# The store of the transposed input moved behind the first index-head rotation, and more urgent PSUM copies of the decays' sums

## The chip, the cores and the metric

The kernel runs on one core of one Trainium2 chip. TensorE (PE) multiplies matrices, VectorE (DVE), ScalarE (ACT) and GpSimd (POOL) work on elements, SyncE (SP) issues almost all DMA transfers. Each engine takes its instructions in one fixed order and waits by semaphores for the others. The time is that of one execution on the device, in microseconds.

## The reference

One layer of a hybrid streaming encoder for two groups of streams that share the weights: a prompt of 512 new frames and a sample group of 64 frames whose first 512 positions lie in a cache. The width is 1024.

```python
mod = (jax.nn.silu(c) @ w_ada + b_ada)[:, None, :]
sh1, sc1, gt1, sh2, sc2, gt2 = jnp.split(mod, 6, axis=-1)
h = rms_normalize(x) * g_norm_mix * (1.0 + sc1) + sh1
q, k, v, qi, ki, wi, z, xbc, dt, gate_logits = jnp.split(h @ w_in, offs, axis=-1)
q = rope(rms_normalize(q.reshape(b, t, N_HEADS, HEAD_DIM)) * g_q, pos)
k = rope(rms_normalize(k.reshape(b, t, N_KV_HEADS, HEAD_DIM)) * g_k, pos)
qi = rope(qi.reshape(b, t, IDX_HEADS, IDX_DIM), pos)
ki = rope(ki[:, :, None, :], pos)[:, :, 0, :]
...
score = jnp.einsum('th,ths->ts', ww.astype(jnp.float32), jax.nn.relu(logits))
score = jnp.where(kpos[None, :] < limit[:, None], score, -jnp.inf)
_, idx = lax.top_k(score, topk)
...
dtp = jax.nn.softplus((dt + dt_bias).astype(jnp.float32))
acs = jnp.cumsum(dtc * a.reshape(g, r), axis=2)
w_state = jnp.exp(acs[:, :, -1:] - acs) * dtc
...
mixed = (g_attn * (o_attn @ w_branch_attn) + g_ssm * (y @ w_branch_ssm)) @ w_out
x = x + gt1 * mixed
```

Eight index heads score all keys, each query keeps its best 128 (prompt) or 144 (sample), attention runs over these, a state-space scan (SSD) runs on another slice of the projection, and both branches are merged, projected and added to x. A SwiGLU block follows. The residual x is needed again near the end; the decays' sums (acs) are needed by the scan.

## The kernel before

The kernel is written as a plain program (`build`), in which every operation is recorded by a planner, `Plan`. Nothing is issued while the program is recorded. `order` then lists the operations: it keeps for each engine a heap of those whose inputs are ready, takes the one of highest urgency, and books a modelled duration (`cost`). The urgency is the place in the program minus an offset, which `with R.prio(n)` sets: `R.prio(4000)` makes an operation as urgent as one that stands 4000 operations earlier, `R.prio(-1500)` less urgent. `with R.after(ops)` adds dependencies for the planner only. `emit` issues everything in the resulting order, so each engine's queue, SyncE's too, is that order. All instructions therefore have one line, L533, in the profile, and are told apart by their tiles. Because one choice shifts all later ones, a small edit changes the order of many operations.

Memory is given out by pools. A pool opens and closes by events that stand in program order: "close" takes effect in the plan once all operations of the pool have been listed, and a later "open" waits behind it. Operations of a pool that isn't open are held. Memory of a closed pool goes to the next pool on its side; an operation on the new tile waits on the chip for the last users of the old one.

The stages around the change, in the order of the program (lines of the kernel before):

- Start (692 to 893). x is loaded (`xt`), normalized and transposed; the modulation's first 2048 columns are computed by `ada_pair`; `h_tile` makes the projection's input in two parts, high (`hTh`) and low (`hTl`), because each product is made of three fast ones. At urgency -1500, lines 870 to 883 transpose the raw x by TensorE into PSUM (`pxt`), copy it to five tiles `xs` in pool `xsp`, and store them to `x_d`, a scratch array in HBM, from which the residual is read near 924 us. These are six stores: four of 512 KB (rows of 512 bytes) and two of 128 KB (rows of 128 bytes).
- `R.close(sp, xsp)` at line 951, then pools "attn" and "index" open. Their first operations load the rope table `cs2`, the gains `gqk`, and for the index keys the cached part: `kd` (named `kisd`), inside `key_stack`. `key_stack` copies the rotated new keys beside the cached ones, transposes them (PSUM tag `px`), and splits them into high and low parts (`kis`, on ScalarE and VectorE).
- Index heads (1072 to 1078). For each half, `tm` projects four heads into `tok`, `rope` rotates them (two products on VectorE into `tmpb`, one on GpSimd, one addition on VectorE, whose operation is kept as `ropes[0]` or `ropes[1]`), and `q_stack` transposes and splits them into `qis`.
- Decays (1081 to 1129). Softplus on VectorE (tiles `e1`, `e2`, `e3`, shown as `e`), then sums by matmuls with a triangular matrix (`pacs` in a `px` bank) and with ones (`ptot` in a `py` bank). `nacs` is the negated first, `edec` the exponential of the second, `wst` their sum. The same sums transposed (`pacsT`) go to `acsT` and to HBM.
- Index scores and top-k (1132 to 1171). Per block of 128 queries: two matmuls per head into a `py` bank, ScalarE's relu into `lg`, VectorE's weighted sum into `score`, then 16 or 18 passes of the eight largest (`m`, by MAX8) and their removal (MATCH_REPLACE8), then a mask.
- Modulation, `ada_columns(4, adx)` (1174 to 1177, held back to `ropes[0]`): four loads `adr` from `w_ada`, 16 accumulations on VectorE (`aacc`), and a few matmuls. Pool "adax" lies on the right side of the memory.
- Keys `kx` and values `vx`: projection, and for the keys `rope` with a normalization (a sum of squares on VectorE into `rr`, a power on GpSimd, a product). Then the queries, fillers, and attention.

Weights stream through two buffers `raw`, and are split into `wh` (ScalarE) and `wl` (VectorE). Fillers are projections of the gates; their weights and matmuls are used wherever the planner has nothing more urgent for TensorE. PSUM has two banks of each tag `px` and `py` and two double banks `mm`.

Of the kernel before, what the change touches and what calls it, by code (L numbers as in the profile page):

```python
# [8 lines left out]
AF = mybir.ActivationFunctionType  # L9
OP = mybir.AluOpType  # L10
# [3 lines left out]
P = 128  # L14
D = 1024
NP_, NS = 512, 64
T = NP_ + NS
TH = T // 2
HP, HS = NP_ // 2, NS // 2
# [521 lines left out]
def build(tc, I, O):  # L541
    R = Plan(tc)
    vec, act, pool, pe, sync = R.vec, R.act, R.pool, R.pe, R.sync
# [5 lines left out]
    xsp = R.mkpool("xs", side="right")  # L549
    sp = R.mkpool("start")  # L550

    def pmm(name):
        return psum.tile([P, 2, 512], F32, name=name, tag="mm", bufs=2)

    def px(name, tag="px"):
        return psum.tile([P, 512], F32, name=name, tag=tag, bufs=2)
# [139 lines left out]
    for tb in range(5):  # L696
        n = P if tb < 4 else NS
        t = sp.tile([P, D], F32, name=f"xt{tb}")
        src = x_p[tb * P:(tb + 1) * P] if tb < 4 else x_s
# [104 lines left out]
    x_d = R.dram([P, 8, 2, TH], F32, name="x_d")  # L804
    rs = sp.tile([P, 5], F32, name="rs")
    pool.memset(rs, 1.0)
    for tb in range(5):
# [5 lines left out]
        for k4 in range(2):  # L813
            p = px(f"pxn{tb}_{k4}")
# [51 lines left out]
    for k4 in range(2):  # L866
        ks = slice(4 * k4, 4 * k4 + 4)
        act.activation(hsS[:, ks, 0:NS], hTh[:, ks, NP_:T].bitcast(F32), AF.Copy)
        act.activation(hsS[:, ks, NS:P], hTl[:, ks, NP_:T].bitcast(F32), AF.Copy)
    with R.prio(-1500):  # L870
        for tb in range(5):
            n = P if tb < 4 else NS
            p = pmm(f"pxt{tb}")
            for kt in range(8):
                pe.transpose(p[:, kt // 4, (kt % 4) * P:(kt % 4) * P + n], xt[tb][:n, kt * P:(kt + 1) * P], ident[:n, :n])
            st = xsp.tile([P, 8, P], F32, name=f"xs{tb}", tag="xs", bufs=5)
            for k4 in range(2):
                vec.tensor_copy(st[:, 4 * k4:4 * k4 + 4, :n], p[:, k4].rearrange("p (k q) -> p k q", k=4)[:, :, :n])
            if tb < 4:
                sync.dma_start(x_d[:, :, tb // 2, tb % 2 * P:tb % 2 * P + P], st)  # L880
            else:
                for hf in range(2):
                    sync.dma_start(x_d[:, :, hf, HP:TH], st[:, :, HS * hf:HS * hf + HS])


    sync.dma_start(rowsB, I["w_conv"][0].rearrange("j (a b) -> (j a) b", b=P))
# [61 lines left out]
            vec.tensor_tensor(out[0:NS, 4, :], out[0:NS, 4, :], p[NS:P, :n], OP.add)  # L948


    R.close(sp, xsp)
    ap_ = R.mkpool("attn", reuse_waits="tile")
    ix = R.mkpool("index", reuse_waits="tile")
    cs2 = ix.tile([P, 5, P], F32, name="cs2")
# [62 lines left out]
    p = px("pmiscT")  # L1017
# [3 lines left out]
    p = px("pmiscS")  # L1021
# [50 lines left out]
    ropes, masked = [], []  # L1072
# [32 lines left out]
    nacs = cp.tile([P, 5, 32], F32, name="nacs")  # L1105
    wst = cp.tile([P, 5, 32], F32, name="wst")
    edec = cp.tile([P, 5, 32], F32, name="edec")
    R.slack = 3.0
    p = px("pacs")
    p2 = px("ptot", "py")  # L1110
# [1 line left out]
        pe.matmul(p[:, 32 * c:32 * c + 32], tri, dA[:, c, :], start=True, stop=True)  # L1112
        pe.matmul(p2[:, 32 * c:32 * c + 32], ones, dA[:, c, :], start=True, stop=True)
    fl = lambda z: z.rearrange("p c h -> p (c h)")
    vec.tensor_scalar(fl(nacs), p[:, :160], -1.0, None, op0=OP.mult)
    act.activation(fl(edec), p2[:, :160], AF.Exp)
    vec.tensor_tensor(fl(wst), p2[:, :160], fl(nacs), OP.add)
    act.activation(wst, wst, AF.Exp)
    vec.tensor_tensor(wst, wst, dtp, OP.mult)
    p = [px("pacsTa"), px("pacsTb", "py")]  # L1120
# [2 lines left out]
        pe.matmul(o, dA[:i0, c, :], tri[:i0, :i0], start=True, stop=True)  # L1123
    R.slack = SLACK
    acsT = ix.tile([32, T], F32, name="acsT")
    act.activation(acsT[:, :NP_], p[0][:32, :], AF.Copy)
    act.activation(acsT[:, NP_:], p[1][:32, :NS], AF.Copy)
    acs_d = R.dram([32, T], F32, name="acs_d")
    sync.dma_start(acs_d, acsT)


    masks = []
# [38 lines left out]
            vec.tensor_copy(masks[b][64:128], masks[b][0:64])  # L1171


    adx = R.mkpool("adax", side="right", reuse_waits="tile")
    for u, op in ((4, ropes[0]),):
        with R.after([op]):
            ada_columns(u, adx)
# [329 lines left out]
    for s, dst in ((0, O["conv_prompt"]), (1, O["conv_sample"])):  # L1507
        p = px(f"pcvo{s}")
# [33 lines left out]
    for a in range(8):  # L1542
# [7 lines left out]
        for c0, n, d0, dn in ((0, NP_, 0, HP), (NP_, NS, HP, HS)):  # L1550
            src = t2(m[:, c0:c0 + n])
# [68 lines left out]
    for hf in range(2):  # L1620
# [4 lines left out]
        p = px(f"pss2{hf}")  # L1625
# [195 lines left out]
    for a in range(8):  # L1821
# [11 lines left out]
        for hf in range(2):  # L1833
# [5 lines left out]
            p = px(f"pyt{a}{hf}", ("px", "py")[hf])  # L1839
# [45 lines left out]
```

## Time and profile before

| what | us |
|---|---|
| median of three runs | 1385.15 (1384.11 to 1385.37) |
| the profiled execution | 1384.84 |
| its span, first to last instruction | 1383.1 |
| busy: PE, DVE, ACT, POOL | 1357.8, 1053.1, 721.3, 246.4 |
| mean granted TensorE clock | 0.999 |

A row of an engine's timeline gives the start, the length, the engine, the operation, the tile written and those read, and in square brackets the idle time before it with what ended it. A row of SyncE gives the issue of a transfer, not its landing. Rows of one kind that follow each other are put together (x6). "a<-b" names tiles without their numbers: `tok` stands for all of a tag.

### The profile page before, as it was taken

Reading aid. Unit: us, or ns where it says so; the run is one execution under the profiler, and the core shown is the slowest. Engines: PE = TensorE matmul, PEld = TensorE weight load, DVE = VectorE, ACT = ScalarE, POOL = GpSimd, SP = SyncE. Lnnn points to the kernel's source line nnn. Section 1 sums busy time; section 2 is a strip of 40 time slices with the busy share of each in tenths; the row PEclk is TensorE's granted clock in tenths of the full one; section 3 lists DMA queues with packets and bytes.
Section 4 is the critical chain, followed back from the end, with each engine's and each line's share of the span. In section 5 each row is a group of like instructions: output and inputs, shape, how many; then the busy total and the mean of one; then the engine's idle time right before and its main releaser. Section 6 shows DMA issues by size and latency. Waiting matters only on the chain.

```text
span 1383.1 us, 27717 instructions
## 1 busy us (share of the span) xinstructions
PE 1357.8 (98%) x10801; PEld 1319.1 (95%) x10801; DVE 1053.1 (76%) x2099; ACT 721.3 (52%) x1496; POOL 246.4 (18%) x366
## 2 busy tenths in 40 slices
PE   7999999999999999999999999999999999999998
PEld 5899999999999999999999999999999999999997
DVE  5579999787778798988887588855998888875221
ACT  5435243777777666666665342225676666661221
POOL 1221012330300355655463200000000000000000
PEclk9999999999999999999999999999999999999999
DMA  9933345674853554444446597755233333246331
GB/s 303 252 109 95 94 128 143 151 177 98 188 143 104 163 144 120 122 140 129 132 127 178 187 332 250 223 173 170 64 107 92 92 96 100 81 135 200 112 105 30
DMA packets 268836, 200.18 MB, mean 145 GB/s; under 512 B 24992, under 2 KB 240192, under 8 KB 268704
## 3 DMA queue, kind: packets, MB, share of 16 engines
q1 hardware_dynamic: 265680, 187.39, 45.9%
q0 software_dynamic: 3024, 11.01, 4.2%
q8 instruction: 85, 1.39, 0.4%
q14 instruction: 47, 0.39, 0.1%
HBM read 157.81 MB, written 29.55 MB: 135 GB/s over the span
## 4 chain that ended last, share of the span: by engine, by line
PE 84%; DVE 7%; DMA 4%; ACT 2%; issue 1%; SPq 1%; POOL 0%; ACTq 0%; DVEq 0%; POOLq 0%
PE mm L533 62%; PE py L533 13%; PE px L533 8%; DVE score L533 1%; DMA stage<-y_d 1%; DVE wl L533 1%; DMA raw<-in_w_in 1%; DVE m L533 1%; SPq L533 1%; DMA xt<-in_x_sample 1%; DVE y L533 0%; DVE xlS L533 0%; DVE qis L533 0%; DMA kd<-in_cache_k 0%; DMA bc<-acs_d 0%
## 5 line engine op out<-in xcount | busy, mean ns | idle before, releaser
L533 ACT ACTIVATE wh<-raw 128x1024 fp32r<-128x1024 f32 (+2 forms) x159 | 156.5, 986 | 237.8 <-PE mm L533 179.6
L533 PE MATMUL mm<-hTh,wh 128*128 128x288 f32 (+1 forms) x1024 | 233.5, 304 | 1.8 <-ACT hTh L533 1.8
L533 PE MATMUL mm<-hTh,wl 128*128 128x288 f32 (+1 forms) x1024 | 234.5, 303 | 0.0
L533 PE MATMUL mm<-hTl,wh 128*128 128x288 f32 (+1 forms) x1024 | 230.0, 301 | 0.3 <-DVE hTl L533 0.3
L533 DVE TENSOR_TENSOR wl<-raw,wh 128x1024 fp32r<-128x1024 f32 (+2 forms) x116 | 139.7, 1205 | 80.7 <-ACT wh L533 75.4
L533 PEld LDWEIGHTS mm<-hTh,wh 128*128 128x128 f32 (+1 forms) x1024 | 166.0, 189 | 5.0 <-ACT hTh L533 2.4
L533 PEld LDWEIGHTS mm<-hTh,wl 128*128 128x128 f32 (+1 forms) x1024 | 167.6, 189 | 2.7 <-issue 1.3
L533 PEld LDWEIGHTS mm<-hTl,wh 128*128 128x128 f32 (+1 forms) x1024 | 165.7, 188 | 2.7 <-issue 1.2
L533 DVE SCALAR_TENSOR_TENSOR cu<-xc,wc,cu 128x579 f32<-128x579 f32 x96 | 83.5, 872 | 2.9 <-ACT cu L533 2.3
L533 PE MATMUL mm<-fh,wh 128*128 128x288 f32 x352 | 80.6, 298 | 0.1
L533 PE MATMUL mm<-fh,wl 128*128 128x288 f32 x352 | 79.7, 298 | 0.9 <-DVE x2r L533 0.9
L533 PE MATMUL mm<-fl,wh 128*128 128x288 f32 x352 | 80.4, 298 | 0.0
L533 PE MATMUL mm<-wl,hTh 128*128 128x256 f32 x256 | 72.2, 283 | 0.6 <-DVE wl L533 0.6
L533 PE MATMUL mm<-wh,hTl 128*128 128x256 f32 x256 | 72.5, 285 | 0.0
L533 PE MATMUL mm<-wh,hTh 128*128 128x256 f32 x256 | 71.3, 283 | 0.0
L533 DVE SCALAR_TENSOR_TENSOR aacc<-adr,sil,aacc 128x512 f32<-128x512 f32 x98 | 68.8, 748 | 1.7 <-DMA adr<-in_w_ada 1.6
L533 PEld LDWEIGHTS mm<-fh,wl 128*128 128x128 f32 x352 | 58.0, 189 | 1.7 <-DVE x2r L533 1.4
L533 PEld LDWEIGHTS mm<-fh,wh 128*128 128x128 f32 x352 | 58.2, 189 | 0.4 <-ACT wh L533 0.3
L533 PEld LDWEIGHTS mm<-fl,wh 128*128 128x128 f32 x352 | 58.1, 189 | 0.5 <-issue 0.4
L533 PE MATMUL mm<-yh,wl 128*128 128x288 f32 x256 | 56.3, 298 | 0.0
L533 PE MATMUL mm<-yh,wh 128*128 128x288 f32 x256 | 55.0, 297 | 0.9 <-ACT yh L533 0.9
L533 PE MATMUL mm<-yl,wh 128*128 128x288 f32 x256 | 54.7, 296 | 0.6 <-DVE yl L533 0.6
(439 smaller groups left out, 3762.8 us busy)
## 6 DMA issues: line engine op xcount, KB each, us to landing
raw<-in_w_in SPq DMA_DIRECT2D x80, 512.0 KB, 4.0
adr<-in_w_ada SPq DMA_DIRECT2D x48, 512.0 KB, 6.0
rawu<-in_w_gate_up SPq DMA_DIRECT2D x22, 512.0 KB, 3.8
raw<-in_w_gate_up SPq DMA_DIRECT2D x22, 512.0 KB, 3.9
wl<-raw POOLq DMA_DIRECT2D x21, 512.0 KB, 5.2
bc<-acs_d SPq DMA_DIRECT2D x32, 256.0 KB, 3.6
raw<-in_w_branch_ssm SPq DMA_DIRECT2D x16, 512.0 KB, 4.9
raw<-in_w_down SPq DMA_DIRECT2D x16, 512.0 KB, 3.7
```

Source lines behind the costliest of these rows:

```text
L533: getattr(engines[x.eng], x.fn)(*[real(a) for a in x.args], **{k: real(v) for k, v in x.kw.items()})
```

## The change

It has two parts. First, the six stores of `xs` are collected in a list and recorded after the store of the decays' sums, with a planner's dependency on the first rotation; the pool of `xs` closes there instead of before "attn", and "adax" opens there and takes the memory of `xs`, so that its tiles wait for the stores. "attn" and "index" now open once the start pool alone is through. Second, the three operations that read `pacs` and `ptot` and the two that read `pacsT` get an urgency of 4000.

```diff
+    xst = []
     with R.prio(-1500):
         for tb in range(5):
...
             if tb < 4:
-                sync.dma_start(x_d[:, :, tb // 2, tb % 2 * P:tb % 2 * P + P], st)
+                xst.append((x_d[:, :, tb // 2, tb % 2 * P:tb % 2 * P + P], st))
             else:
                 for hf in range(2):
-                    sync.dma_start(x_d[:, :, hf, HP:TH], st[:, :, HS * hf:HS * hf + HS])
+                    xst.append((x_d[:, :, hf, HP:TH], st[:, :, HS * hf:HS * hf + HS]))
...
-    R.close(sp, xsp)
+    R.close(sp)
     ap_ = R.mkpool("attn", reuse_waits="tile")
     ix = R.mkpool("index", reuse_waits="tile")
...
-    vec.tensor_scalar(fl(nacs), p[:, :160], -1.0, None, op0=OP.mult)
-    act.activation(fl(edec), p2[:, :160], AF.Exp)
-    vec.tensor_tensor(fl(wst), p2[:, :160], fl(nacs), OP.add)
+    with R.prio(4000):
+        vec.tensor_scalar(fl(nacs), p[:, :160], -1.0, None, op0=OP.mult)
+        act.activation(fl(edec), p2[:, :160], AF.Exp)
+        vec.tensor_tensor(fl(wst), p2[:, :160], fl(nacs), OP.add)
     act.activation(wst, wst, AF.Exp)
     vec.tensor_tensor(wst, wst, dtp, OP.mult)
...
-    act.activation(acsT[:, :NP_], p[0][:32, :], AF.Copy)
-    act.activation(acsT[:, NP_:], p[1][:32, :NS], AF.Copy)
+    with R.prio(4000):
+        act.activation(acsT[:, :NP_], p[0][:32, :], AF.Copy)
+        act.activation(acsT[:, NP_:], p[1][:32, :NS], AF.Copy)
     acs_d = R.dram([32, T], F32, name="acs_d")
     sync.dma_start(acs_d, acsT)
+
+    with R.after([ropes[0]]):
+        for dst, src in xst:
+            sync.dma_start(dst, src)
+    R.close(xsp)
+    adx = R.mkpool("adax", side="right", reuse_waits="tile")
...
-    adx = R.mkpool("adax", side="right", reuse_waits="tile")
     for u, op in ((4, ropes[0]),):
```

Both kernels issue the same instructions; on every engine only their order differs. TensorE's order differs from its 427th matmul on and is the same again in the last third; SyncE's differs from the stores on.

## The prediction

> **What bounds the kernel now.** I read the page first (busy shares, slices, chain), then a table by stage, then TensorE's waits, then the rows of SyncE's queue, VectorE and GpSimd to which those waits point.
>
> ```profile
> PE 1357.8 (98%) x10801; PEld 1319.1 (95%) x10801; DVE 1053.1 (76%) x2099; ACT 721.3 (52%) x1496; POOL 246.4 (18%) x366
> PE   7999999999999999999999999999999999999998
> PE 84%; DVE 7%; DMA 4%; ACT 2%; issue 1%; SPq 1%; POOL 0%; ACTq 0%; DVEq 0%; POOLq 0%
> ```
>
> TensorE is busy 98% of the span and 84% of the chain. No matmul is added or taken away, so the change can win or lose only where TensorE stands still. The table by stage (window, length, then busy time of PE, PEld, DVE, ACT, POOL with their instructions, the granted clock, the DMA share, GB/s) says where that is:
>
> ```profile
> 40.00:52.00 12.00, 11.92 (x128) 10.80 (x129) 4.51 (x13) 5.91 (x13) 2.28 (x6) 1.00 0.94 263
> 52.00:60.00 8.00, 5.84 (x47) 5.63 (x45) 4.75 (x9) 2.39 (x5) 2.22 (x4) 1.00 0.82 175
> 116.00:160.00 44.00, 44.00 (x370) 43.31 (x370) 40.91 (x91) 16.82 (x32) 3.69 (x2) 1.00 0.24 67
> 194.00:400.00 206.00, 205.66 (x1548) 201.24 (x1547) 165.86 (x428) 132.28 (x276) 46.10 (x40) 1.00 0.61 148
> ```
>
> The clock is full. From 194 to 400 us TensorE lacks 0.34 us, from 116 to 160 nothing, from 52 to 60 it lacks 2.2. Its waits from 40 to 200 us (what waited, on what, total, times, longest):
>
> ```profile
> PE px L533 <- DMA kisd<-in_cache_ki: 2.3, 1, 2.3
> PE py L533 <- DVE wst L533: 1.0, 1, 1.0
> PE px L533 <- DVE kis L533: 0.9, 1, 0.9
> PE py L533 <- ACT lg L533: 0.6, 1, 0.6
> PE mm L533 <- DVE wl L533: 0.6, 1, 0.6
> ```
>
> I call them A (the cached index keys, 2.3, ending near 60 us), B (a bank of the key stack, 0.9, near 70), C (a weight split, 0.6, near 92), D (the decays' sums, 1.0) and E (a bank of index scores, 0.6); 5.4 us in all.
>
> **The moved stores.** SyncE's queue before (start, length):
>
> ```profile
> 42.70 0.43 SPq L533 DMA_DIRECT2D rowsC<-in_state_conv  x1
> 43.17 8.84 SPq L533 DMA_DIRECT2D x_d<-xs  x6
> 52.11 1.58 SPq L533 DMA_DIRECT2D cs<-in_rope  x1
> 53.73 0.43 SPq L533 DMA_DIRECT2D gqk<-in_g_q  x1
> 54.21 1.36 SPq L533 DMA_DIRECT2D gqk<-in_g_k  x1
> 55.67 0.93 SPq L533 DMA_DIRECT2D kisd<-in_cache_ki  x2
> 75.67 1.50 SPq L533 DMA_DIRECT2D raw<-in_w_in  x2
> 77.22 1.02 SPq L533 DMA_DIRECT2D adr<-in_w_ada  x2
> 91.73 1.87 SPq L533 DMA_DIRECT2D raw<-in_w_in  x2
> ```
>
> The six stores hold the queue for 8.84 us. In the changed order rope table, gains and cached keys follow rowsC directly, so the keys' loads leave at 46.8 instead of 55.7. A goes (2.3), with some 6 us to spare; the filler matmuls that follow have their weights. B hangs on VectorE's queue: the subtraction that frees the bank stands behind the softplus chain of small instructions. In the changed order it stands three of them further forward, and its input comes earlier. I count B as gone (0.9).
>
> The dependency on the rotation steers the planner alone. No semaphore comes of it, since a store reads nothing that the rotation writes. In the changed order the six stores follow the pair of weight loads of the 75.67 row and precede the modulation's first load (77.22 row): their 8.84 us fall at about 74 to 83 us. Behind them are queued that load, the next two weight loads, and the second modulation load. The modulation's buffers now lie in the memory of the stored copy, so its first load waits in earnest until the fourth store has landed:
>
> ```profile
> x_d<-xs SPq DMA_DIRECT2D x4, 512.0 KB, 5.8
> DMA to landing us min/median/max: 3.9/7.2/7.9
> ```
>
> The second line is the modulation's loads. A store issued at 79 lands at 85, the load behind it leaves at 85 and lands at 89 (3.9) to 93 (7.9). Its users on VectorE:
>
> ```profile
> 89.02 0.88 DVE L533 TENSOR_SCALAR aacc<-adr,sil 128x512 f32<-128x512 f32 x2
> 89.82 0.74 DVE L533 SCALAR_TENSOR_TENSOR aacc<-adr,sil,aacc 128x512 f32<-128x512 f32 x1
> 90.48 1.22 DVE L533 TENSOR_TENSOR wl<-raw,wh 128x1024 fp32r<-128x1024 f32 x1
> 98.82 1.49 DVE L533 TENSOR_TENSOR tok<-tok,tmpb 128x1280 f32<-128x1280 f32 x1 [2.85 <-POOL tok L533]
> ```
>
> Before, three accumulations delayed the split (90.48) that C waits for. In the changed order this split comes straight behind the query stack: 1.6 us leave its path and C (0.6) goes. The three accumulations now stand ahead of the next rotation's last addition (98.82), for which VectorE had 2.85 us of idle time. With 3.8 us won that addition is due at 95.0, and the accumulations must start by 93.4. The bounds are 0 (landed at 89) and, at the latest landing, 1 us with queueing; I take 0, since 93 is still inside.
>
> **The more urgent copies.** Their durations do not change. On VectorE before:
>
> ```profile
> 110.21 0.33 DVE L533 TENSOR_SCALAR nacs<-px 128x160 f32<-128x160 f32 x1
> 110.45 0.74 DVE L533 SCALAR_TENSOR_TENSOR aacc<-adr,sil,aacc 128x512 f32<-128x512 f32 x1
> 111.11 0.32 DVE L533 TENSOR_TENSOR wst<-py,nacs 128x160 f32<-128x160 f32 x1
> 111.49 0.53 PE L533 MATMUL py<-kis,qis 128*128 128x288 f32 x2 [0.96 <-DVE wst L533]
> ```
>
> An accumulation stands between the copy and the addition, and in the changed order it still does. On ScalarE the exponential and the two transposed copies move a few places forward; nothing on TensorE waited for them (bounds: 0 to the 1.0 of D). With 3.8 us won and two accumulations fewer ahead (1.5), the addition ends at 111.43 - 3.8 - 1.5 = 106.1. TensorE comes to the bank 12 matmuls sooner in its order (1.4 us), at 110.53 - 3.8 - 1.4 = 105.3. D stays at 0.8 to 1.0: nothing won, nothing lost.
>
> **Where the gain meets VectorE.** VectorE is full from here to E (40.91 of 44 us above): index scores and top-k passes.
>
> ```profile
> 122.39 1.49 DVE L533 TENSOR_TENSOR kx<-kx,rr 128x1280 f32<-128x1280 f32 x1 [2.50 <-POOL rr L533]
> 124.49 0.82 DVE L533 TENSOR_TENSOR tmpb<-kx,tabs 128x640 f32<-128x640 f32 x1
> 175.31 0.41 DVE L533 TENSOR_SCALAR score<-lg,wi 128x384 f32<-128x384 f32 x1
> 176.30 0.62 PE L533 MATMUL py<-kis,qis 128*128 128x384 f32 x2 [0.61 <-ACT lg L533]
> ```
>
> From the addition's end (111.43) to that score (175.31) are 63.9 us. In the changed order the keys' rotation leaves this stretch: its product (1.49), one partial product (0.82), two small instructions (at 0.3 each, like the 110.21 row), the 2.50 us wait for GpSimd; and one weight split fewer stands in it (1.2). That is 6.6 us less, 57.3; I take 58, as VectorE is partly paced by the matmuls there. The score then starts at 106.1 + 58 = 164.1 and the bank is served 0.99 later, as before, at 165.1. TensorE arrives at 175.69 - 3.8 less the 67 matmuls that the changed order puts behind this point (7.9 us at 44 us for 370): 164.0. E grows from 0.6 to 1.1.
>
> The sum: TensorE passed this point at 176.30; now at 165.1 with 7.9 us more left to do, as if 173.0. Net **-3.3 us**: A, B and C give 3.8, E takes 0.5 back.
>
> The keys' rotation must go somewhere: it now stands among the last top-k passes, right ahead of attention.
>
> ```profile
> 118.81 3.55 POOL L533 TENSOR_TENSOR rr<-rr,mhalf 128x20 f32<-128x20 f32 x1 [20.02 <-DVE rr L533]
> 181.17 3.19 POOL L533 TENSOR_TENSOR kx<-kx,tabs 128x1280 f32<-128x1280 f32 x1 [45.11 <-DVE tmpb L533]
> 187.89 1.59 POOL L533 COPY kd<-kx 128x640 f32<-128x640 f32 x1 [1.31 <-issue]
> 246.27 0.27 PE L533 MATMUL px<-ident,kd 128*128 128x128 f32 x1
> 251.11 0.34 PE L533 MATMUL py<-kst,qst 128*128 128x128 f32 x2
> ```
>
> Before, the keys' copy was done at 189.5, 57 us before their last transpose. That cover is spent: product, partial products, GpSimd's 3.19, addition, copy are now 9.4 us in series, ending shortly ahead of attention's first product (251.11), which the changed order puts 41 matmuls (4.9 us) later. I count nothing for it, since TensorE has filler matmuls in that order; without the cover it is up to the 9.4. Behind attention the orders converge, and their last third is the same; for other interleavings until there I allow 1 us either way, three times what TensorE lacks from 194 to 400.
>
> **The forecast.** The profiled execution took 1384.84 us (span 1383.1), 0.3 below the median of 1385.15. 1384.84 - 3.3 = 1381.5.
>
> **The rivals.**
> 1. The gain is given back at E, no change. If VectorE's stretch shortens by 3 us instead of 6, because waits for ScalarE and TensorE take the place of the work that left, TensorE waits the difference at E. Against it: VectorE was 93% busy there. 1384 to 1386.
> 2. Slower: the keys' rotation becomes a wait ahead of attention, at the transposes of keys and first queries. The price is the part of the 9.4 us series that filler does not cover, with GpSimd's 3.55 us power of the first queries beside it. It decides from 3.3 us on; at 4 to 10 us the time is 1385.5 to 1391.5. For it: a cover of 57 us shrinks to a few. Against it: attention's first product is placed later too, behind filler.
> 3. The stores' drain holds up the loads queued behind them. Their issue took 1.5 us each against 0.4 for a small load, so the queue feels the drain. The next weights leave behind a modulation load at 85 us or later; before, they left at 91.73, so they have 7 us in hand less the 3.8 that TensorE is early. Beyond that every microsecond counts: +1 to +4 on the forecast, 1382.5 to 1385.5. The Trainium skill, "DMA: Bandwidth & Descriptors", section "Queues, rings and completion order", has each engine's copies taken from its rings in order, which speaks against this change: every load behind the stores is late by their whole drain. By that rule the weights land behind all six stores, near 90; no run here has shown that order with the stores at this place.
> 4. More: D goes too and E does not bind: -4.2 to -5.4, 1379.4 to 1380.6.
>
> **How the numbers follow.** Chances: the forecast 0.46, rival 4 0.10, rival 1 0.12, rival 2 0.24, rival 3 0.08. The predicted time is the forecast's, 1381.5; its own range, with the terms of 1 us, 1380.3 to 1382.8. The range of 8 in 10 reaches from rival 4's middle to rival 2's middle: 1379.8 to 1388.5. A measurement of this kernel can hardly tell 0.2% (2.8 us) from no change: faster is under 1382.4, slower over 1387.9. Rival 4, four fifths of the forecast and a little of rival 3 give faster 0.48; the rest of the forecast, rivals 1 and 3 and 0.06 of rival 2 give same 0.33; the rest of rival 2 gives slower 0.19.
>
> **What would show it.** Right: no wait for the cached keys; none for the weight split near 92 us; the six stores in the queue at 74 to 83 us; the wait for the decays' sums as before; one wait of about a microsecond for a score bank near 165 us. Wrong: TensorE waiting for keys or queries near 245 us (rival 2); VectorE waiting for a modulation load near 90 us and then TensorE for a rotated tile, or ScalarE for weights and then TensorE (rival 3); a wait of over 3 us at the score bank (rival 1).

## The result, and the profile after

The changed kernel took 1390.25 us (median of six runs, 1388.57 to 1391.86) where the kernel before took 1384.94 (six runs): a ratio of 1.0037, interval 1.0027 to 1.0048. It is slower by 5.3 us, above the range that I gave. Two later measurements of the same kernel gave 1.0026 (1.0015 to 1.0037) and 1.0034 (1.0021 to 1.0047).

The page of the profiled execution (span 1388.4 us, beside 1383.1), the shares and the chain:

```profile
PE 1362.3 (98%) x10801; PEld 1320.6 (95%) x10801; DVE 1066.5 (77%) x2099; ACT 722.0 (52%) x1496; POOL 244.9 (18%) x366
PE 79%; DVE 7%; DMA 6%; ACT 3%; issue 2%; SPq 1%; POOL 1%; ACTq 0%; POOLq 0%; DVEq 0%
```

VectorE issues the same 2099 instructions and is busy 13.4 us longer. That is the first sign: something on it was stretched. The table by stage of the kernel after, in the prediction's windows and one more:

```profile
52.00:60.00 8.00, 8.00 (x66) 8.00 (x65) 4.85 (x9) 4.81 (x8) 3.21 (x4) 1.00 0.53 153
116.00:160.00 44.00, 43.55 (x354) 43.30 (x353) 43.97 (x106) 14.62 (x25) 0.14 (x1) 1.00 0.30 86
250.00:400.00 150.00, 145.15 (x1082) 139.40 (x1081) 119.03 (x314) 109.86 (x243) 35.62 (x29) 1.00 0.58 139
```

and the last window in the kernel before:

```profile
250.00:400.00 150.00, 149.66 (x1124) 145.24 (x1123) 114.02 (x313) 110.00 (x244) 33.43 (x30) 1.00 0.62 148
```

The hole at 52 to 60 us is filled. A new one of 4.9 us is between 250 and 400 us, where TensorE had lacked 0.34. TensorE's waits from 40 to 400 us in the kernel after:

```profile
PE px L533 <- DVE P L533: 3.2, 2, 1.6
PE mm L533 <- DMA wl<-raw: 1.3, 1, 1.3
PE px L533 <- ACT wh L533: 0.6, 1, 0.6
PE py L533 <- ACT lg L533: 0.5, 1, 0.5
PE px L533 <- DVE tok L533: 0.5, 1, 0.5
PE mm L533 <- DVE wl L533: 0.5, 1, 0.5
PE mm L533 <- ACT hTh L533: 0.4, 1, 0.4
PE py L533 <- DVE wst L533: 0.3, 1, 0.3
```

A and B are gone, D is 0.3 us, E is 0.5; the wait for a split that is left is a later one, at 140 us. Largest are two waits of 1.6 us for P, the softmax weights of attention. They were not among the waits before. Their rows, first the transposes that wait:

```profile
264.09 0.52 PE L533 MATMUL px<-ident,P 128*128 128x128 f32 x2 [1.59 <-DVE P L533]
292.80 0.88 PE L533 MATMUL px<-ident,P 128*128 128x128 f32 x4 [1.60 <-DVE P L533]
```

then the VectorE instructions of the kernel after that take longer than their like (they account for 10.9 of the 13.4 us),

```profile
91.56 3.56 DVE L533 TENSOR_SCALAR aacc<-adr,sil 128x512 f32<-128x512 f32 x2 [0.22 <-DMA adr<-in_w_ada]
226.38 4.21 DVE L533 TENSOR_SCALAR mask<-score 128x512 bf16<-128x512 f32 x1
261.31 3.31 DVE L533 TENSOR_SCALAR P<-P,sm 128x128 f32<-128x128 f32 x4
290.39 3.38 DVE L533 TENSOR_SCALAR P<-P,sm 128x384 f32<-128x384 f32 x4
```

the same instructions in the kernel before (the accumulations stand in the prediction, at 89.02: 0.88),

```profile
244.34 0.42 DVE L533 TENSOR_SCALAR mask<-score 128x512 bf16<-128x512 f32 x1
260.94 0.87 DVE L533 TENSOR_SCALAR P<-P,sm 128x128 f32<-128x128 f32 x4
281.64 1.39 DVE L533 TENSOR_SCALAR P<-P,sm 128x384 f32<-128x384 f32 x4
```

and GpSimd in the kernel after:

```profile
91.48 2.96 POOL L533 TENSOR_TENSOR tok<-tok,cs 128x1280 f32<-128x1280 f32 x1 [11.51 <-DVE tmpb L533]
227.03 3.26 POOL L533 TENSOR_TENSOR kx<-kx,tabs 128x1280 f32<-128x1280 f32 x1
261.04 2.90 POOL L533 TENSOR_TENSOR tok<-tok,tabs 128x1280 f32<-128x1280 f32 x1 [1.45 <-DVE sm L533]
289.60 2.93 POOL L533 TENSOR_TENSOR tok<-tok,tabs 128x1280 f32<-128x1280 f32 x1 [3.10 <-DVE tmpb L533]
```

In each of the four cases VectorE's instruction begins within a microsecond of a rotation's product on GpSimd, and is through within 1.3 us of that product's end (261.04 + 2.90 = 263.94; the scalings that need 0.87 us end at 264.62). All four are scalings with one input, in SBUF (the mask, which compares each score with one number, is the same operation). Instructions with two inputs are booked by the planner on a port shared with GpSimd (`op.port` in `add`); these are not, so the planner does not keep them clear of the product that a partial product shortly ahead of them has released. The Trainium skill, "SBUF — State Buffer", section "Who interferes with whom", states such a lock for VectorE's scalings and copies in a two-port mode: whoever comes first has the port for the whole instruction. Three of the rows agree: GpSimd begins there first. The profile names no mode, but the scalings cost 0.53 ns a column (0.87 us for four of 128, 1.68 for four of 512), half the 1.03 of VectorE's operation with two inputs (0.51 us for 288 columns, 0.74 for 512). The mask's row does not agree by itself: it begins 0.65 us before the product, while GpSimd was issuing a DMA (from 226.22, 1.07 us), and yet lasts until the product is over. Nor is every GpSimd instruction such a neighbour. Beside GpSimd's power of 128x20, the scalings of another block took no longer than elsewhere (1.68 us for four, 1.67 in a run where nothing lay beside them):

```profile
286.28 3.72 POOL L533 TENSOR_TENSOR rr<-rr,mhalf 128x20 f32<-128x20 f32 x1 [8.77 <-DVE rr L533]
288.67 1.68 DVE L533 TENSOR_SCALAR P<-P,sm 128x512 f32<-128x512 f32 x4
```

To see the sum, I went through TensorE's matmuls and took for each the time to the next one beyond what is usual for its kind (the median interval, 0.3 us at most), added these up, and compared the kernels where equal work was done. The numbers are us lost against the kernel before, at the times of the kernel before, counted from its 55 us mark; the last column is what had been lost up to 55 us, where TensorE's order is nearly the same in all:

```
kernel, run             80     120     250     300     480     560     900     end   up to 55
changed               -3.6    -5.5    -4.1    +1.6    +1.8    +3.2    +5.2    +4.4       +1.6
changed, third time   -3.6    -5.5    -4.1    +3.4    +3.6    +5.1    +7.9    +7.4       +1.5
changed, scalings and
 mask first           -3.6    -5.5    -4.1    -0.9    -0.8    +0.7    +1.0    +0.4       +1.4
before, stores in gap -3.6    -3.6    -3.5    -3.5    -3.4    -3.4    -3.1    -3.2       +2.9
before, one product
 beside scalings      -0.3    -0.3    -0.3    +2.1    +2.2    +2.2    +2.9    +2.1       +0.9
```

By this count the change wins 4.1 us by 250 us (TensorE's waits alone give 3.6 there, and 4.0 at 120, where the count is rough since the two orders hold different matmuls), loses 5.7 between 250 and 300, and some 3 after that. The start's 1 to 3 us are scatter between executions: the modulation's first load left at 7.79 us in the profile before, at 8.87 in the changed kernel's.

The two rows of the changed kernel, one program, part at 300 us. There the granted clock of TensorE differs, here in the third profile and then in the first (the column before the last two):

```profile
295.00:300.00 5.00, 5.00 (x25) 4.47 (x25) 3.80 (x9) 3.81 (x11) 0.00 (x0) 0.69 0.81 191
295.00:300.00 5.00, 5.00 (x36) 4.72 (x35) 5.00 (x13) 3.88 (x11) 0.00 (x0) 1.00 0.82 202
```

The same 5 us hold 25 matmuls instead of 36. By the clock that is (1 - 0.69) x 5 = 1.6 us, an estimate, of the 1.8 between the rows. Such a dip came again in the third profile from 836 to 842 us (0.72, so 1.7 us), behind a wait of 1.9 us for the tile `yh`. In the fourteen profiles every dip from 40 us on, but for the program's last 3 us, begins within 2 us of the end of a wait of TensorE of 1.6 to 5.0 us; waits of up to 2.3 us also passed without one. So a wait can cost more than its own length, and profiles of one kernel differ by it.

### The profile page after: what moved, and what is told of

It reads as the page before. It is cut to its first block, busy times and chain, and to the rows that moved or that the text cites. A ratio compares the mean times of both kernels' runs of the same rounds, so it can differ in the third digit from the quotient of the medians.

```text
span 1388.4 us, 27743 instructions
## 1 busy us (share of the span) xinstructions
PE 1362.3 (98%) x10801; PEld 1320.6 (95%) x10801; DVE 1066.5 (77%) x2099; ACT 722.0 (52%) x1496; POOL 244.9 (18%) x366
## 4 chain that ended last, share of the span: by engine, by line
PE 79%; DVE 7%; DMA 6%; ACT 3%; issue 2%; SPq 1%; POOL 1%; ACTq 0%; POOLq 0%; DVEq 0%
PE mm L533 58%; PE py L533 12%; PE px L533 8%; DMA stage<-y_d 2%; DVE score L533 2%; DMA raw<-in_w_in 1%; SPq L533 1%; DVE m L533 1%; DVE wl L533 1%; DMA bc<-acs_d 1%; DMA xt<-in_x_sample 1%; ACT wh L533 1%; DMA wl<-raw 1%; DVE aacc L533 1%; DMA x_d<-xs 0%
## 5 line engine op out<-in xcount | busy, mean ns | idle before, releaser
L533 PE MATMUL mm<-hTl,wh 128*128 128x288 f32 (+1 forms) x1024 | 234.1, 303 | 0.0
L533 DVE TENSOR_TENSOR wl<-raw,wh 128x1024 fp32r<-128x1024 f32 (+2 forms) x116 | 142.7, 1233 | 70.1 <-ACT wh L533 67.5
L533 DVE SCALAR_TENSOR_TENSOR cu<-xc,wc,cu 128x579 f32<-128x579 f32 x96 | 89.8, 936 | 3.0 <-ACT cu L533 2.2
```

The source lines that it names most:

```text
L533: getattr(engines[x.eng], x.fn)(*[real(a) for a in x.args], **{k: real(v) for k, v in x.kw.items()})
```

## The experiments

**The stores alone, planned anew.** The second part of the change is taken back.

```diff
-    with R.prio(4000):
-        vec.tensor_scalar(fl(nacs), p[:, :160], -1.0, None, op0=OP.mult)
...
+    vec.tensor_scalar(fl(nacs), p[:, :160], -1.0, None, op0=OP.mult)
...
```

> The first part alone: the six stores moved and the pools closed later, no urgency for the copies of the decays' sums. The theory that VectorE's scalings of P are held by GpSimd's products at 261 and 290 us says nothing on the place of the stores as such: this kernel loses where its order happens to set a one-input VectorE instruction beside a GpSimd product just ahead of a TensorE need, so anything from 1382 to 1390. The rival that the moved stores and the late keys' rotation cost by themselves expects 1388 to 1391, as the whole change. If the urgency is what turned a gain into a loss, 1381 to 1384.

Measured: 1389.70, ratio 1.0022 (1.0012 to 1.0032). It loses without the urgency too, and again TensorE waits 1.6 us for P, once. That wait is not what makes this kernel slow: by the count of the table its profile is still 1.5 us ahead at 300 us and 3.6 behind at the end, with waits of 1.6 and 0.8 us between 600 and 800 us for the tiles `sto` and `r`. In this order the loss lies in the stretch that no run took apart. The wait for the decays' sums is 0.3 us here too, so its fall comes of the new order and not of the urgency. The urgency alone, on the kernel before, leaves every engine's order as it was. It can matter only on top of the moved stores, and the loss doesn't need it.

**The stores alone, all else in the order before.** The orders are taken as planned before and the six stores moved by hand; the same is done in the next runs.

```diff
         self.order()
+        # the six stores, "close xs" and "open adax" go ahead of the first load of adr
+        at = next(i for i, x in enumerate(seq) if self.tile_of(x) == "wada4_0")
+        self.seq = seq[:at] + moved + events + seq[at:]
```

> The order of the kernel before on every engine, with only the six stores taken from their place and put ahead of the modulation's first load. My prediction's steps A and B hold if this is 2.3 to 3.3 us faster than before: 1381.6 to 1382.7, and TensorE no longer waits for the cached keys. The rival that the stores' drain costs what it saves expects 1384 to 1387, with waits for weights or for the modulation's loads between 80 and 110 us.

Measured: 1389.47, ratio 1.0021 (1.0012 to 1.0030): slower, where I expected a gain. SyncE's and VectorE's rows of this run:

```profile
75.77 10.02 SPq L533 DMA_DIRECT2D x_d<-xs  x6
87.99 1.81 SPq L533 DMA_DIRECT2D adr<-in_w_ada  x2
91.99 0.88 DVE L533 TENSOR_SCALAR aacc<-adr,sil 128x512 f32<-128x512 f32 x2 [4.45 <-DMA adr<-in_w_ada]
```

and TensorE's largest wait:

```profile
PE mm L533 <- DVE wl L533: 5.0, 1, 5.0
```

The waits A and B are gone. But the modulation's load left at 88 instead of 77 us, VectorE stood 4.45 us before its accumulations, and the weight split queued behind them held TensorE for 5.0 us. Behind this wait the granted clock was 0.66 from 94 to 99 us, worth 1.7 us more by estimate; 5.0 and 1.7 less the 3.2 of A and B are 3.5, near the 3.1 measured. This is the rival of the stores' drain, at its full price. In the changed kernel the planner had put the split ahead of the accumulations, and there this wait does not occur.

**The scalings of P ahead of GpSimd's product.** In the changed kernel, the last partial product and GpSimd's product that it releases go behind the scalings, at two places.

```diff
         self.order()
+        for rb, prod, last in (("q1rb", "q1", "a00P3"), ("q2rb", "q2", "a02P3")):
+            # a: last partial product into rb, b: GpSimd's product into prod, z: scaling of last
+            self.seq = seq[:at] + [a, b] + seq[at:]      # at: right behind z
```

> The changed kernel with one thing moved at two places: the last partial product of the rotation of the second and third queries, and GpSimd's product that it releases, come behind the four scalings of P instead of ahead of them. The port theory: the two groups of scalings fall from 3.3 to about 0.9 and 1.4 us, TensorE's two waits of 1.6 us for P go, 1386.8 to 1387.5. The rival that attention starts late because keys and queries are late: P is late anyway, under 1 us won, 1389.5 to 1390.5.

Measured: 1388.52, ratio 1.0014 (1.0005 to 1.0023). The scalings are back at their usual length and both waits for P are gone. Against the kernel before on the same chip this is 2.1 us slower, where the changed kernel was 3.6 to 5.1 by its ratios. In its profile, though, the wait for a weight's low part near 253 us was 2.0 us instead of 1.3, and behind it the granted clock was 0.66 from 256 to 261 us (1.7 us by estimate), so in this one execution the stretch from 250 to 300 us lost about as much as before.

**And the mask too.**

```diff
-        for rb, prod, last in (("q1rb", "q1", "a00P3"), ("q2rb", "q2", "a02P3")):
+        for rb, prod, last in (("krb", "kx", "mask3"), ("q1rb", "q1", "a00P3"), ("q2rb", "q2", "a02P3")):
```

> As the run before it, and also the last mask (4.21 us beside GpSimd's product of the keys at 227 us, 0.42 in the kernel before) comes ahead of the partial product that releases this product. The port theory: VectorE is done some 3 to 4 us sooner with its stretch ahead of attention, and the wait for a weight's low part near 253 us may go too: 1384.5 to 1387. The rival, that this mask has slack: no difference to the run before.

Measured: 1387.47, ratio 1.0015 (1.0005 to 1.0025). The mask took 0.43 us instead of 4.21, but the product then met an instruction shortly behind it, which took 0.41 us in the kernel before:

```profile
225.48 0.43 DVE L533 TENSOR_SCALAR mask<-score 128x512 bf16<-128x512 f32 x1
227.16 3.13 DVE L533 TENSOR_TENSOR vst<-vx,vst 128x256 fp32r<-128x256 f32 x1
```

VectorE won 1.1 us there instead of 3.8. Beside the run before it the time tells no difference, and whether the mask had slack was not told.

**The changed kernel again.**

> The changed kernel once more, unaltered, as a measure on the same chip for the three beside it. All theories: 1388.5 to 1391.5. In its profile the two scalings of P stand at 3.3 us again beside GpSimd's products; if the wait for a weight's low part near 253 us and the loss of the first 40 us differ from the first profile of it, these two are scatter from execution to execution and no part of the change.

Measured: 1390.05, ratio 1.0026 (1.0015 to 1.0037). The two waits for P are 1.6 us each again; the wait for the low part was 1.7, and some 1.6 us were lost by 55 us as in the first profile. So the late low part belongs to this order, and its size varies.

**The loads ahead of the stores, the stores staying.**

```diff
         self.order()
+        # cs2, gqk, kisd right behind "open attn", "open index", then the six stores
+        self.seq = keep[:at] + opened + loads + stores + closed + keep[at:]
```

> The order of the kernel before with five loads moved: rope table, gains and cached index keys are issued ahead of the six stores, which otherwise stay where they were (with the pools of attention and index opened before them). The theory that the gain is in these loads alone, and that the stores at 75 us only cost because the modulation's loads queue behind them: the wait for the cached keys (2.3 us) and the one for the key stack (0.9) go, nothing else moves: 2.3 to 3.3 us faster than before. The rival that the cached keys would only be waited for elsewhere: 0 to 1 us.

Measured: 1385.85, ratio 0.9992 (0.9984 to 1.0001), as the rival has it. Wait A is gone, and two others took its place. SyncE, ScalarE and TensorE of this run:

```profile
50.06 9.87 SPq L533 DMA_DIRECT2D x_d<-xs  x6
60.03 1.33 SPq L533 DMA_DIRECT2D raw<-in_w_in  x1
65.16 1.06 ACT L533 ACTIVATE wh<-raw 128x1024 fp32r<-128x1024 f32 x1 [5.18 <-DMA raw<-in_w_in]
69.37 0.66 PE L533 MATMUL px<-ident,kisd 128*128 128x128 f32 x4 [1.59 <-POOL kisd L533]
```

The next weight load left at 60.0, after the stores, where it left at 54.9 in the changed kernel; 1.6 of these 5.1 us are this execution's later start. Its split reached VectorE late, the rotation of the new index keys stood behind it, and TensorE waited 1.6 us for their copy and 1.3 for the stack.

**The output's key stores later.** The kernel with all three moves, and the two stores of `kx` six weight loads later.

```diff
+        out = [x for x in seq if x.eng == "sync" and x.args[1].base.name == "kx"]
+        self.seq = seq[:at] + out + seq[at:]             # at: behind the sixth load of raw after them
```

> As the kernel with all three scalings ahead of GpSimd's products, and also the two stores of the keys to the output, issued at 233 us between weight loads, come several weight loads later. If the wait for a weight near 253 us is from the traffic that the late keys bring there, it falls from 0.7 to 2.0 us to under 0.3, and the time is about 1 us under the kernel without this edit. If it is GpSimd's queue or ScalarE's that holds the weight, nothing changes.

Measured: 1385.61, ratio 0.9999 (0.9988 to 1.0010), but with a spread of 1384.89 to 1394.51; its profiled execution was the slowest. In that profile the wait for the low part is not smaller:

```profile
PE mm L533 <- DMA wl<-raw: 2.4, 1, 2.4
```

So the traffic of the keys is not shown to be its cause. In this profile the low part's DMA left at 249.02 us and was waited for until 256.94; in the changed kernel it left at 250.40, after ScalarE had stood 3.92 us for the weight itself, and was waited for until 254.99. The granted clock fell three times in this slowest execution (24 to 32 us 0.57, 256 to 262 and 836 to 842 0.72), 6.8 us by estimate. The lower median is within the scatter of the runs without this edit.

**The planner told of the port.**

```diff
-        op.port = eng == "gpsimd" and wide > 0 and fn != "dma_start" or eng == "vector" and wide > 1
+        op.port = (eng == "gpsimd" and wide > 0 and fn != "dma_start" or eng == "vector" and wide > 1
+                   or eng == "vector" and wide == 1 and fn in ("tensor_scalar", "tensor_copy") and not any(is_psum(v) for v in ins + outs))
```

> The changed kernel with one line of the planner altered: it now books VectorE's scalings and copies with one input in SBUF on the port that it shares with GpSimd, as it does those with two inputs. It makes another order from the first microseconds on. The port theory: no scaling of P or mask is stretched beside a GpSimd product any more, and the 300 us mark is reached 3 us sooner than in the changed kernel; the whole time 1384 to 1388, with the scatter of a new order on top (2 us either way). The rival that these stretched instructions were covered: 1388 to 1391.

Measured: 1387.33, ratio 1.0013 (1.0001 to 1.0024). The mask took 0.42 us, but one scaling of P still took 2.08 us, and TensorE did not wait for it. A second group of scalings took 2.25 instead of 1.41, and the operation into `vst` behind the mask 3.05 instead of 0.41. Two new waits of 1.2 and 1.0 us came from the new order; the first, at the transposes of the keys, is of the kind that the prediction's rival 2 feared. So the booking moved the meetings and did not end them; the planner's clock isn't the chip's.

**The stores in the queue's gap.** As the run with the stores alone, but ahead of the two weight loads.

```diff
-        at = next(i for i, x in enumerate(seq) if self.tile_of(x) == "wada4_0")
+        at = next(i for i, x in enumerate(seq) if self.tile_of(x) == "raw7")
```

> The order of the kernel before on every engine, with only the six stores moved: behind the store of the index keys and ahead of the weight loads at 73.7 us, where SyncE's queue stood empty for 10 us in the run with the stores alone. The theory that the stores cost through what is queued behind them: no load waits for them there, TensorE's waits for the cached keys and for the key stack go (2.3 and 0.9 us) and nothing takes their place, 2.5 to 3.6 us faster than before. The rival that the stores' traffic itself slows the loads beside it, wherever it lies: 0 to 1 us faster.

Measured: 1381.61, ratio 0.9971 (0.9961 to 0.9981): 3.9 us faster than before, and faster than both kernels. Its SyncE rows,

```profile
64.73 0.51 SPq L533 DMA_DIRECT2D out_ki_sample<-misc  x1
65.29 9.34 SPq L533 DMA_DIRECT2D x_d<-xs  x6
75.15 1.53 SPq L533 DMA_DIRECT2D raw<-in_w_in  x2
76.78 1.43 SPq L533 DMA_DIRECT2D adr<-in_w_ada  x2
```

and TensorE's waits above 0.5 us:

```profile
PE py L533 <- DVE wst L533: 1.0, 1, 1.0
PE py L533 <- ACT lg L533: 0.6, 1, 0.6
PE mm L533 <- DVE wl L533: 0.6, 1, 0.6
```

The six stores fill the queue until 74.6, and the loads behind them leave within a microsecond of where they left before. A and B are gone, C, D and E are as they were, and of the 3.6 us won at 80 us 3.2 are still there at the end.

**One product beside the scalings, in the kernel before.**

```diff
         self.order()
+        seq = seq[:at] + [partial, product] + seq[at:]   # at: the reciprocal ahead of a00P's scalings
```

> The order of the kernel before, in which GpSimd's product of the second queries' rotation, and the partial product that releases it, are put right ahead of the four scalings of P in attention's first block (they stood some 5 us earlier), and the rotation's addition behind them. Nothing else moves. The port theory: the four scalings take 3 us instead of 0.87, TensorE waits about 1.5 us for P there, and the whole is 1 to 2 us slower than before. The rival that the scalings of the changed kernel were slow for another reason: 0.9 us for the four and no wait.

Measured: 1387.89, ratio 1.0013 (1.0004 to 1.0022), 1.8 us. GpSimd, VectorE and TensorE:

```profile
260.63 2.93 POOL L533 TENSOR_TENSOR tok<-tok,tabs 128x1280 f32<-128x1280 f32 x1 [2.75 <-DVE sm L533]
260.93 3.30 DVE L533 TENSOR_SCALAR P<-P,sm 128x128 f32<-128x128 f32 x4
263.70 0.52 PE L533 MATMUL px<-ident,P 128*128 128x128 f32 x2 [1.02 <-DVE P L533]
```

The same four scalings, 0.87 us before, take 3.30 with nothing changed but the place of the product, of the partial product that releases it and of the addition behind it, and TensorE waits 1.0 us for them and 0.9 for the next step of the block. So the meeting alone makes the wait.

**Scalings and mask first, beside the changed kernel on one chip.**

> The changed kernel with the last mask and the two groups of scalings ahead of GpSimd's products, once more, on the same chip as the changed kernel itself. The port theory: 2.5 to 3.5 us faster than the changed kernel beside it, so about 0.1% slower than the kernel before. The rival: within 1 us of the changed kernel.

> The changed kernel once more, as the measure for the run beside it: 1388 to 1391.

Measured: 1387.68 (ratio 1.0014, 1.0005 to 1.0023) and 1390.28 (1.0034, 1.0021 to 1.0047). Taking the two meetings at P away, with the third moved from the mask to the operation into `vst` (3.13 us here too), is worth 2.6 us; the changed kernel has five runs here, and the two intervals just touch. In the loss table it is 4.3 at the 300 us mark against the changed kernel of the same chip (-0.9 and +3.4), of which 1.6 are that profile's dip of the clock, and 2.5 against the first profile. The kernel is still 0.14% slower than the one before.

## Why the prediction was wrong

*A, B and C go, 3.8 us.* Right. By 80 us the changed kernel had won 3.6 us against the 55 us mark. The keys' loads left at 47.09 us, the prediction had 46.8.

*The stores and what is queued behind them.* The size was off by a little and the place right: the queue was held for 10.24 us from 75.25, not 8.84 from 74. The modulation's load was in use at 91.56, inside my 89 to 93. The next weights left behind the stores, at 88.30, and TensorE did not wait for them. I took 0 for it with 1 as the bound; TensorE waited 0.5 for a rotated tile. That wait came of the accumulations at 91.56, stretched by GpSimd's product from 0.88 to 3.56. The runs show that the zero hung on the planner's new order: with the old order the same place costs 5.0.

```profile
75.25 10.24 SPq L533 DMA_DIRECT2D x_d<-xs  x6
87.70 0.38 SPq L533 DMA_DIRECT2D adr<-in_w_ada  x1
```

*D stays.* Too high: D fell from 1.0 to 0.3. *E grows to 1.1.* It was 0.5, where it had been 0.6. The bank was served at 165.91; taking off the 1.6 us of the start, this is 164.3, where I had 165.1. For the forecast net of -3.3 the table has -4.1 by 250 us.

*The keys' rotation: "I count nothing for it, since TensorE has filler matmuls in that order".* This held as far as it went: TensorE did not wait for the keys or the queries. Rival 2, the slower side, has the measured time in its range of 1385.5 to 1391.5, but by luck, since the wait that it prices did not occur.

*"For other interleavings until there I allow 1 us either way".* This is the step that failed. The bound was taken from TensorE's idle time in the old order, 0.34 us from 194 to 400, which says nothing of what a new order sets side by side. 5.7 us were lost from 250 to 300 us. 3.2 of them are the two waits for P. In the kernel before, the rotations of the second and third queries had their GpSimd products at 255.35 and 295.32 us, clear of the scalings of P at 260.94 and 281.64; in the changed order the products stand at 261.04 and 289.60, beside the scalings at 261.31 and 290.39, on which attention's transposes wait with nothing between. The keys' own product met the mask, for which TensorE is not seen to wait. That the meetings make the waits is shown by taking them away and by making one in the kernel before. 1.3 to 1.7 us more are the wait for a weight's low part near 253 us.

*The orders converge behind attention.* They do, but the stretch until then was not free: in the changed order's profiles 1.3 to 4 us more were lost from 300 us to the end, some 1.5 of it in each between 480 and 560, and 1.7 of the 4 by a dip of the clock. So the allowance failed here too.

One small slip besides: terms of 1 us around 1381.5 give 1380.5 to 1382.5, not 1380.3 to 1382.8, and nothing hangs on it.

Two things stay open, and together they are about as large as what is shown. Why the low part of a weight is late near 253 us: it is not shown to be the keys' traffic. And the loss after 300 us: it appears in every profile of the new order and comes of no single wait (the largest between 500 and 600 us is 0.5 us, for the scan's scaled inputs; near 835 us it is 1.1 for `yh`, 0.9 in the kernel before), and no run took it apart.

## What to carry to other kernels

When a change shifts an order that a planner writes, ask not only what waits for what, but what will now run beside what: beside a GpSimd product of 128x1280, VectorE's scalings with their operands in SBUF took 2.0 to 3.8 us longer here, about the product's 3 us. Before a transfer is moved in a queue, look for the gap in that queue and for the loads behind it: the same six stores were worth -3.9 us in a gap of 10 us, and +3.1 when they came 10 us later. Take the order before as it is and move one thing by hand; this separated the gain of a change from the chance effects of a new order. And when a repair leaves the neighbour where it is, look at what it meets next.

## What the runs showed that I had not expected

The order of a list scheduler carries several microseconds of its own: the stores alone, planned anew, were 1.0022, the same stores in the old order 0.9971 to 1.0021 by their place.

Single executions scatter by more than I had taken from three runs (1384.11 to 1385.37). On the three chips of the experiments the kernel before ran from 1383.20 to 1390.62, and in the profiles of the experiments up to some 3 us are lost in the first 55 us against the profile before, where the order of the matmuls is nearly the same in all.

Six stores held the queue for 8.84, 9.34, 9.87, 10.02 and 10.24 us in five profiles; no run shows what sets the length, so a place in the queue must have room for the longest.
